# Gate products in pages of 512 columns with four buffers, paced by half weight pages at first, and readout pages read back half a page later

## Chip, cores and metric

The kernel runs on one NeuronCore of a Trainium2 chip. The metric is the device time of one execution in microseconds; 2185.92 is the median of three runs before the change. An execution is also profiled, and all rows below come from that one profiled execution. Engines are named as the profile names them: PE (TensorE), PEld (its weight loads), DVE (VectorE), ACT (ScalarE), POOL (GpSimd), SP (SyncE, which here only issues DMAs).

## The reference, cut to what matters

One layer of a hybrid block over 512 latent tokens (and 256 context tokens), D = 2048, DFF = 5632:

```
s_c = silu(c);  mx = split(s_c @ w_ada + b_ada, 6)          # six gate / shift / scale vectors of 2048
h   = modulate(rms_norm(x), mx[0], mx[1]);  u = h @ w_in    # also for the context, SSM columns only
pool groups: windowed means of u[:1536] - u, then @ w_pool
SSM groups:  B_bar u, bidirectional scan (context gives the start state), readout with C
mix = concat(pool, gelu(ssm) * sigmoid(gelu(ssm) @ w_glu)) @ w_out
x   = x + mx[2] * rms_norm(mix)
f   = conv_glu_ffn(modulate(rms_norm(x), mx[3], mx[4])) ;  x = x + mx[5] * rms_norm(f)
```

All large products are made in float32 precision from pairs of fp32r values (a high part and a remainder), three matmuls for one.

## The kernel before, in words

**Weight pages.** Every weight matrix is streamed in pages of 128x1024 floats (512 KB) in one fixed list. `Stream.get` hands out page i. Ahead of that, it makes page i+1 (an ACT copy to `whi` at L77, and a DVE subtraction to `wlo` at L78) and issues the load of page i+2 on SP (L60). The ring holds two raw pages, two `whi` and two `wlo`; so the load of page i+2 waits until `wlo` of page i is made, and `wlo` of page i+1 until PE is through with page i-1. Pages are counted here from 0 in the order of the list: 8 to 31 are w_in for the pool channels (`ub`), 40 to 65 are w_out and w_glu (`wo`, `glu`), 66 to 73 the last quarter of w_out (`wo2`, made into `wbh` and `wbl` up to three pages ahead), then w_up and w_down. A `wo` page is 24 matmuls of 128x512.

**Background threads.** Everything else is written as Python generators that `Threads.tick` steps between the matmuls of a page, twice or more a page, until a budget of microseconds (the first number that a generator yields) is used up. The second number is a lag: the thread isn't stepped again before so many pages have passed. A low priority number goes first. The steps only fix the order of instructions on each engine's queue; each engine then works its queue strictly in order, and SP does so too.

**Gate products.** Gates mx[2], mx[3], mx[4] (c = 0, 1, 2) are made as dot products on DVE: `gemv` (L963), thread of lowest priority, loads rows of w_ada as pages `gv` of 128x1024 (512 KB, SP, L172, two buffers) and multiplies each with `srow` in one SCALAR_TENSOR_TENSOR that sums into `gacc` (L972). The load of page x+1 stands just ahead of dot x, and must wait until dot x-1 has freed its buffer. The first 7 rows of c = 0 come another way (`gpair_dot`, L607); `gemv` makes 82 dots. Gate mx[5] is made likewise in the FFN stage (`gemv5`, 32 dots, L1253), one page apart and not loaded ahead.

**Readout of the SSM.** `front` (thread of priority 0) runs the SSM. Its last part is a loop over u (L845, eight groups), one half of an iteration for each half weight page:

```
        for u in range(11):
            if u < 8:
                eb_mm(u)
            if 1 <= u <= 8:
                mi_load(u - 1)
            if 2 <= u <= 9:
                y_mm(u - 2)
```

After a yield of half a page the second half follows: `window(u+1)` (ACT, from POOL's `cl`, feeds `eb_mm(u+1)`), `e_out(u)`, `y_act`, `cl_build(u+2)` (SP loads `cu` and `du`, DVE and POOL products). `e_out(u)` copies the bank to `E` (ACT), adds `du` on DVE (L828) and writes `E` to DRAM (`e_scratch`, ACT's queue); `mi_load(u)` (L832) reads it back in another layout on SP as `Mi`, and so waits on SP until the write has landed; `y_mm(u)` on PE uses `Mi`.

**Stages.** 0 to 172 us: statistics, modulation, SSM input products. 172 to 372: w_in pages with pooling, scan on DVE. 372 to 595: w_out pages, with readout (435 to 531) and gate products. 595 to 720: `wo2`, first norm, start of w_up. From 720: FFN, 1463 us.

Of the kernel before, what the change touches and what calls it, by code (L numbers as in the profile page):

```python
# [21 lines left out]
F32 = mybir.dt.float32  # L22
# [4 lines left out]
OP = mybir.AluOpType  # L27
# [102 lines left out]
def emit(tc, A, out, xs_dram, dbg=None):  # L130
    nc = tc.nc
    V, S, PO, PE = nc.vector, nc.scalar, nc.gpsimd, nc.tensor
# [4 lines left out]
    ring = es.enter_context(tc.tile_pool(name="ring", bufs=1))  # L137
# [22 lines left out]
    def pg(name, shape=(1024,), dt=F32, parts=128):  # L160
        return shaped(sb.tile([128, 1024], dt, name=name, tag="pg", bufs=NPG), shape, slice(0, parts))

    def bank(name, cols=512, parts=128):
        t = ps.tile([128, 512], F32, name=name, tag="bank")
        return t[:parts, :cols]

    def cst(name, shape, dt=F32):
        return sb.tile(shape, dt, name=name, tag=name)

    def gvload(ap, q=None):  # L170
        r = ring.tile([128, 1024], F32, name="gv", tag="gv", bufs=2)
        nc.sync.dma_start(r[:], ap)  # L172
        return r

# [42 lines left out]
    pa = phA.enter_context(tc.tile_pool(name="pa", bufs=1))  # L217
# [8 lines left out]
    srow = pa.tile([128, 2048], F32, name="srow")  # L226
    ident = cst("ident", [128, 128])
    nc.scalar.dma_start(ident[:], A["ident"])
    pscol = cst("pscol", [128, 12])
    rcnt = cst("rcnt", [128, 4, 16])  # L230
    hmask = cst("hmask", [128, 16])
    sbr = pg("sbr", (2, 32, 16))
    BBt = pa.tile([128, 1040], F32, name="bb")
# [10 lines left out]
    scr = cst("scr", [128, 1024], BF)  # L244
# [188 lines left out]
        early.setdefault(r, []).append(f)  # L433

    ada = {}
    gacc = cst("gacc", [128, 2, 4, 16])

    def ada_round(R):

# [127 lines left out]
    def mi_build(k, t, tmp):  # L567
        g0 = 4 * k
        m = t.rearrange("p (r g i h) -> p r g i h", r=2, g=4, i=8)
        for _ in cmul_build(m[:, 0], m[:, 1], BB[:, 0, g0:g0 + 4, :], BB[:, 1, g0:g0 + 4, :], PIN, g0, 4, PO, tmp):  # L570
            pass
        return m
# [31 lines left out]
    def gpair_dot(nt):  # L604
        g = gpair.pop(nt)
        for hf in range(2):
            V.scalar_tensor_tensor(scr[:], g[:, hf], 1.0, srow[:, hf * 1024:(hf + 1) * 1024], op0=OP.mult,  # L607
                                   op1=OP.mult, accum_out=gacc[:, hf, 0, nt:nt + 1])

    NGP = 7  # L610
    at(31, cond_rows)
# [68 lines left out]
    def front():  # L680
        def mi_next(k):
            if k < 8:
                cm = pb.tile([128, 512], F32, name="cm", tag="cm", bufs=1)
                mis[k] = mi_build(k, pb.tile([128, 1024], F32, name="mi", tag="mi", bufs=1)[:], cm[:])

        for gb in range(4):
# [5 lines left out]
                                        ap=[[768, 8], [6144, 16], [1, 768]]), uc.rearrange("p i c -> p (i c)"))  # L692
        mi_next(NMT)
        yield 0.0, 1.0
        for gb in range(4):
            u = pg(f"UT{gb}", (8, NCH))
            UT[gb] = u
            nc.sync.dma_start(u, bass.AP(tensor=u_dram.tensor, offset=gb * 128 * 768,
                                         ap=[[96, 8], [6144, 16], [768, 8], [1, 96]]))
            yield 0.0, 0.5 if gb < 3 else 0.75  # L700
        for gb in range(4):
            for kk in range(2):
                k = 2 * gb + kk
                g0 = 4 * k
                if k >= NMT:
                    for r in range(2):
                        mt_half(k, r)
                    mi_next(k + 1)
                    yield 0.0, 0.4
                mt = mts.pop(k)  # L710
                for r in range(2):
                    bp = bank("bp", 4 * NCH)
                    for g in range(4):
                        PE.matmul(bp[:, g * NCH:(g + 1) * NCH], mt[:, r, g, :], UT[gb][:, (g0 + g) % 8, :],
                                  start=True, stop=True)
# [116 lines left out]
        def mi_load(u):  # L832
            Mis[u] = mi = pc.tile([128, 4, 8, 16], F32, name="Mi", tag="Mi", bufs=2)
            nc.sync.dma_start(mi[:].rearrange("p g j h -> p g (j h)"),
                              bass.AP(tensor=e_dram.tensor, offset=u * 32 * 960,
                                      ap=[[16, 8], [960, 16], [240, 4], [1, 128]]))
# [8 lines left out]
        for u in range(11):  # L845
            if u < 8:
                eb_mm(u)
            if 1 <= u <= 8:
                mi_load(u - 1)
            if 2 <= u <= 9:  # L850
                y_mm(u - 2)
            if u >= 4 and u % 2 == 0:
                yt_mm(u // 2 - 2)
            yield 0.0, 0.5
            if u < 7:
                window(u + 1)
# [103 lines left out]

    gv_state = [0]

    def gemv():  # L963
        todo = [(c, n, hf) for c in range(3) for n in range(16) for hf in range(2)][2 * NGP:]
        tiles = []
        for x in range(len(todo)):

            while len(tiles) < min(x + 2, len(todo)):
                c, nt, hf = todo[len(tiles)]
                tiles.append(gvload(A["ada_n"][c, nt, hf]))  # L970
            c, nt, hf = todo[x]
            V.scalar_tensor_tensor(scr[:], tiles[x][:], 1.0, srow[:, hf * 1024:(hf + 1) * 1024], op0=OP.mult,  # L972
                                   op1=OP.mult, accum_out=gacc[:, hf, c, nt:nt + 1])
            tiles[x] = None
            gv_state[0] = 2 * NGP + x + 1
            if nt == 15 and hf == 1:
                gfin(c)
            yield 1.4, 0

    def gfin(c):  # L980
        a = acol[:, c, :]
        V.tensor_tensor(a, gacc[:, 0, c, :], gacc[:, 1, c, :], op=OP.add)
        V.tensor_tensor(a, a, bcol[:, 2 + c, :], op=OP.add)
        if c in (0, 3):
            V.tensor_tensor(a, a, gcol[:, 1 if c == 0 else 3, :], op=OP.mult)
# [68 lines left out]
    def second_half():  # L1054

        bg.finish(phs["scan"], fr_t)
        pcx["es"].close()
        P3["es"] = ExitStack()
        P3["p"] = p3 = P3["es"].enter_context(tc.tile_pool(name="p3", bufs=1))
        P3["arow"] = [t.rearrange("p (a b) -> p a b", a=2) for t in (BBt[:, :1024], PIOt[:])]  # L1060
        while gv_state[0] < 32:
            bg._step(gv_t)
        glu()
        P3["ar_t"] = bg.add(rows_of(0, P3["arow"], p3, "dg", 1), 0)

# [179 lines left out]
    def gemv5():  # L1245
        for hf in range(2):
            sr = p2.tile([128, 1024], F32, name="srow2", tag="srow2", bufs=1)
            nc.sync.dma_start(sr[:], A["c_row"][:, hf * 1024:(hf + 1) * 1024])
            S.activation(sr[:], sr[:], AF.Silu)
            for nt in range(16):  # L1250
                r = gvload(A["ada_n"][3, nt, hf])
                yield 0.0, 1
                V.scalar_tensor_tensor(scr[:], r[:], 1.0, sr[:], op0=OP.mult, op1=OP.mult,  # L1253
                                       accum_out=gacc[:, hf, 3, nt:nt + 1])
                yield 1.2, 0
        gfin(3)
        yield from rows_of(3, frow, p2, "srow2", 1)

# [133 lines left out]
    r = None  # L1392
    for t in range(4):
# [25 lines left out]
        r = rows_rstd(st8[:, t:t + 1, :], 0, 4)[0]  # L1419
# [88 lines left out]
```

## Time and profile before

| | before |
|---|---|
| median of 3 runs (lowest, highest) | 2185.92 us (2182.75, 2189.2) |
| the profiled execution's own time | 2184.42 us |
| its span, first to last instruction | 2182.6 us |
| PE busy | 2073.6 us (95%) |
| DVE busy | 1545.1 us (71%) |
| ACT / POOL busy | 690.7 / 261.7 us |
| mean granted PE clock | 0.978 |
| bytes read from HBM | 302.46 MB |

Busy is the time in which an engine had an instruction under way. The granted clock is the share of full speed (2.4 GHz) that PE got; in a stretch between 0.5 and 1 it is a mean over 1.2 and 2.4 GHz.

### The profile page before, as it was taken

How to read it: one execution, taken by the hardware profiler on the slowest of the kernel's cores; microseconds unless marked ns; L12 is line 12 of the kernel's file. 1: busy time of each engine (PE TensorE's matmuls, PEld its weight loads, DVE VectorE, ACT ScalarE, POOL GpSimd, SP SyncE). 2: the span in 40 equal slices, each digit the busy share in tenths (PEclk: the TensorE clock that was granted, in tenths of full speed). 3: DMA queues.
4: the chain of work that ended last, by engine and by line, in shares of the span. 5: the costliest groups of instructions: out<-in, count | busy, mean ns of one | idle time of the engine just before them, and what ended most of it. 6: DMA issues, size and time to landing. Idle time of an engine off the chain costs nothing.

```text
span 2182.6 us, 24482 instructions
## 1 busy us (share of the span) xinstructions
PE 2073.6 (95%) x9468; PEld 1639.6 (75%) x9468; DVE 1545.1 (71%) x2135; ACT 690.7 (32%) x969; POOL 261.7 (12%) x318
## 2 busy tenths in 40 slices
PE   7997999788798999999999999999999999999996
PEld 3576877566587888888888888888888888888885
DVE  1576899655667688767777777777766767767676
ACT  4343325433256323322222222222222222222224
POOL 5951100262016000000000000000000000000004
PEclk8899999899998999999999999999999999999998
DMA  9877423666656233333333433333322322333225
GB/s 380 302 285 258 167 85 121 211 186 193 211 205 229 68 97 116 118 123 116 123 110 116 135 116 117 125 114 114 102 90 93 97 95 90 96 96 97 90 95 192
DMA packets 94292, 315.00 MB, mean 144 GB/s; under 512 B 16992, under 2 KB 22880, under 8 KB 89952
## 3 DMA queue, kind: packets, MB, share of 16 engines
q1 hardware_dynamic: 90848, 306.07, 42.3%
q10 hardware_dynamic: 3328, 7.37, 0.9%
q8 instruction: 74, 1.21, 0.2%
q14 instruction: 42, 0.34, 0.0%
HBM read 302.46 MB, written 10.94 MB: 144 GB/s over the span
## 4 chain that ended last, share of the span: by engine, by line
PE 74%; DMA 10%; DVE 10%; issue 3%; ACT 3%; POOL 1%; SPq 0%; ACTq 0%; DVEq 0%; POOLq 0%
PE up L176 14%; PE up L178 14%; PE up L177 14%; PE dn L178 7%; PE dn L177 7%; PE dn L176 7%; DMA gv<-in_ada_n 5%; DVE wlo L78 2%; DVE scr L972 2%; DVE sct L664 1%; PE ada L446 1%; DVE B L665 1%; DMA e_scratch<-E 1%; ACT scr L1086 1%; DMA raw<-in_w_up 1%
## 5 line engine op out<-in xcount | busy, mean ns | idle before, releaser
L78 DVE TENSOR_TENSOR wlo<-raw,whi 128x1024 fp32r<-128x1024 f32 (+1 forms) x326 | 407.3, 1250 | 362.8 <-ACT whi L77 359.8
L77 ACT ACTIVATE whi<-raw 128x1024 fp32r<-128x1024 f32 (+1 forms) x326 | 341.4, 1048 | 795.0 <-PE dn L178 313.2
L1274 DVE SCALAR_TENSOR_TENSOR cv<-zp,wconv,cv 128x512 f32<-128x512 f32 x704 | 528.1, 750 | 18.8
L176 PE MATMUL up<-h,whi 128*128 128x512 f32 x1344 | 531.4, 395 | 0.0
L177 PE MATMUL up<-h,whi 128*128 128x512 f32 x1344 | 530.8, 395 | 0.0
L178 PE MATMUL up<-h,wlo 128*128 128x512 f32 x1344 | 530.8, 395 | 0.0
L178 PEld LDWEIGHTS up<-h,wlo 128*128 128x128 f32 x1344 | 251.9, 187 | 61.8
L177 PEld LDWEIGHTS up<-h,whi 128*128 128x128 f32 x1344 | 251.9, 187 | 61.5
L176 PEld LDWEIGHTS up<-h,whi 128*128 128x128 f32 x1344 | 251.9, 187 | 61.4
L178 PE MATMUL dn<-whi,g 128*128 128x512 f32 x672 | 265.5, 395 | 0.0
L176 PE MATMUL dn<-whi,g 128*128 128x512 f32 x672 | 265.5, 395 | 0.0
L177 PE MATMUL dn<-wlo,g 128*128 128x512 f32 x672 | 265.5, 395 | 0.0
L1088 POOL TENSOR_TENSOR facc<-facc,frow 128x512 f32<-128x512 f32 x11 | 15.4, 1423 | 1434.9 <-ACT scr L1086 1434.9
L972 DVE SCALAR_TENSOR_TENSOR scr<-gv,srow 128x1024 bf16<-128x1024 f32 x82 | 114.1, 1392 | 86.6 <-DMA gv<-in_ada_n 86.3
L1308 ACT ACTIVATE zp<-up 128x512 f32<-128x512 f32 x84 | 50.5, 601 | 378.6 <-PE up L178 378.6
L177 PEld LDWEIGHTS dn<-wlo,g 128*128 128x128 f32 x672 | 126.0, 187 | 30.8
L178 PEld LDWEIGHTS dn<-whi,g 128*128 128x128 f32 x672 | 126.0, 187 | 30.8
L176 PEld LDWEIGHTS dn<-whi,g 128*128 128x128 f32 x672 | 126.0, 187 | 30.8
L177 PE MATMUL wo<-wlo,mx 128*128 128x512 f32 x192 | 81.3, 424 | 32.1 <-DVE wlo L78 32.1
L1322 DVE TENSOR_TENSOR facc<-facc,dn 128x512 f32<-128x512 f32 x144 | 92.1, 680 | 0.7 <-PE dn L178 0.7
L178 PE MATMUL ub<-hT,wlo 128*128 128x512 f32 x192 | 77.2, 402 | 11.9 <-DVE wlo L78 11.9
L176 PE MATMUL wo<-whi,mx 128*128 128x512 f32 x192 | 80.5, 419 | 0.0
(276 smaller groups left out, 2441.9 us busy)
## 6 DMA issues: line engine op xcount, KB each, us to landing
raw<-in_w_up SPq DMA_DIRECT2D x176, 512.0 KB, 3.6
gv<-in_ada_n SPq DMA_DIRECT2D x114, 512.0 KB, 4.5
raw<-in_w_down SPq DMA_DIRECT2D x88, 512.0 KB, 3.6
adak<-in_ada_k SPq DMA_DIRECT2D x32, 1024.0 KB, 8.6
raw<-in_w_out SPq DMA_DIRECT2D x32, 512.0 KB, 5.0
raw<-in_w_inp SPq DMA_DIRECT2D x24, 512.0 KB, 4.9
adag<-in_ada_n SPq DMA_DIRECT2D x7, 1024.0 KB, 8.7
xl<-in_xT SPq DMA_DIRECT2D x8, 512.0 KB
```

Of the source, the lines that this page charges most:

```text
L77: nc.scalar.activation(hi[:, :n], raw[:, :n], AF.Copy)
L78: nc.vector.tensor_tensor(lo[:, :n], raw[:, :n], hi[:, :n].bitcast(F32), op=OP.subtract)
L176: PE.matmul(o, ahi, bhi, start=start, stop=False)
L177: PE.matmul(o, ahi, blo, start=False, stop=False)
L178: PE.matmul(o, alo, bhi, start=False, stop=stop)
L446: PE.matmul(ada[q, w][32 * g:32 * g + 32, :], scol[:, 4 * j + g, :], t[:, g, :], start=j == 0, stop=j == 3)
L664: V.tensor_tensor(tv, y[:, :, r], p[:, sl].unsqueeze(1).to_broadcast([128, n, 2, 32]), op=OP.mult)
L665: V.tensor_tensor(x, x, tv, op=OP.add)
L972: V.scalar_tensor_tensor(scr[:], tiles[x][:], 1.0, srow[:, hf * 1024:(hf + 1) * 1024], op0=OP.mult, op1=OP.mult, accum_out=gacc[:, hf, c, ...
L1274: V.scalar_tensor_tensor(a[:], zz, wcol, a[:], op0=OP.mult, op1=OP.add)
L1308: S.activation(zp[j][i % 2][:, 1:9, 1:65], o.rearrange("p (r c) -> p r c", r=8), AF.Copy)
L1322: V.tensor_tensor(f, f, os[t], op=OP.add)
```

## The change

`gv` pages have 512 columns (256 KB), four buffers, and are loaded three pages ahead of their dot. `gacc` has four columns of partial sums for each output instead of two; it is cleared at the start, and `gfin` has one more addition. A step of `gemv` is a half-size dot with a cost of 0.68; until the front thread has made its last `mi` page (k == 7) it also has a lag of half a weight page, afterwards none. `gemv5` uses the same generator, half a page apart. `mi_load(u - 1)` moves from the first half of iteration u to the head of its second half. `rcnt` moves to the pool that is closed ahead of the FFN.

```
-    def gvload(ap, q=None):
-        r = ring.tile([128, 1024], F32, name="gv", tag="gv", bufs=2)
+    gv_lag = [0.5]
+
+    def gvload(ap):
+        r = ring.tile([128, 512], F32, name="gv", tag="gv", bufs=4)
         nc.sync.dma_start(r[:], ap)
...
-    gacc = cst("gacc", [128, 2, 4, 16])
+    gacc = cst("gacc", [128, 4, 4, 16])
+    V.memset(gacc[:], 0.0)
...
                     mi_next(k + 1)
+                    if k == 7:
+                        gv_lag[0] = 0
                     yield 0.0, 0.4
...
             if u < 8:
                 eb_mm(u)
-            if 1 <= u <= 8:
-                mi_load(u - 1)
             if 2 <= u <= 9:
                 y_mm(u - 2)
...
             yield 0.0, 0.5
+            if 1 <= u <= 8:
+                mi_load(u - 1)
...
+    def gv_dots(todo, row):
+
         tiles = []
         for x in range(len(todo)):
...
+            while len(tiles) < min(x + 4, len(todo)):
+                c, nt, qf = todo[len(tiles)]
+                tiles.append(gvload(A["ada_n"][c, nt, qf // 2][:, qf % 2 * 512:qf % 2 * 512 + 512]))
+            c, nt, qf = todo[x]
+            V.scalar_tensor_tensor(scr[:, :512], tiles[x][:], 1.0, row(qf), op0=OP.mult,
+                                   op1=OP.mult, accum_out=gacc[:, qf, c, nt:nt + 1])
             tiles[x] = None
+            yield x
+
+    def gemv():
+        todo = [(c, n, qf) for c in range(3) for n in range(16) for qf in range(4)][4 * NGP:]
+        for x in gv_dots(todo, lambda qf: srow[:, qf * 512:(qf + 1) * 512]):
...
-            yield 1.4, 0
+            yield 0.68, gv_lag[0]
...
+        V.tensor_tensor(gacc[:, 0:2, c, :], gacc[:, 0:2, c, :], gacc[:, 2:4, c, :], op=OP.add)
```

The order of instructions on each engine shows what the steps make of it. On SP, in the readout, two rounds of the loop stand in the queue before as follows (`raw` a weight page, `Mi` the read-back, `gv` gate pages, `cu` and `du` the operands of `cl_build`):

```order
L60 DMA raw<-in_w_out 128x1024
L834 DMA Mi<-e_scratch 128x4x128
L172 DMA gv<-in_ada_n 128x1024 x2
L790 DMA cu<-in_ssm_c 128x2x64
L792 DMA du<-in_ssm_d 128x16
L60 DMA raw<-in_w_out 128x1024
L834 DMA Mi<-e_scratch 128x4x128
```

and in the changed kernel:

```order
L174 DMA gv<-in_ada_n 128x512 x4
L60 DMA raw<-in_w_out 128x1024
L839 DMA Mi<-e_scratch 128x4x128
L795 DMA cu<-in_ssm_c 128x2x64
L797 DMA du<-in_ssm_d 128x16
L174 DMA gv<-in_ada_n 128x512 x5
L60 DMA raw<-in_w_out 128x1024
L839 DMA Mi<-e_scratch 128x4x128
```

Gate pages still stand behind `Mi`, but each is loaded three dots ahead. On DVE, the same rounds before:

```order
L78 TENSOR_TENSOR wlo<-raw,whi 128x1024
L972 SCALAR_TENSOR_TENSOR scr,gacc<-gv,srow 128x1024 x2
L828 TENSOR_TENSOR E<-E,du 128x16
L800 TENSOR_TENSOR cm<-cu,pio 128x512
L802 TENSOR_TENSOR cm<-cu,pio 128x512
L78 TENSOR_TENSOR wlo<-raw,whi 128x1024
```

and in the changed kernel:

```order
L78 TENSOR_TENSOR wlo<-raw,whi 128x1024
L833 TENSOR_TENSOR E<-E,du 128x16
L805 TENSOR_TENSOR cm<-cu,pio 128x512
L807 TENSOR_TENSOR cm<-cu,pio 128x512
L976 SCALAR_TENSOR_TENSOR scr,gacc<-gv,srow 128x512 x5
L78 TENSOR_TENSOR wlo<-raw,whi 128x1024
```

The addition into `E` now stands ahead of the round's dots, right behind `wlo`. The third place is DVE in the `wo2` stage (`macc` the running sums that take a `wq` bank); before:

```order
L78 TENSOR_TENSOR wbl<-raw,wbh 128x1024
L972 SCALAR_TENSOR_TENSOR scr,gacc<-gv,srow 128x1024
L78 TENSOR_TENSOR wbl<-raw,wbh 128x1024
L972 SCALAR_TENSOR_TENSOR scr,gacc<-gv,srow 128x1024 x2
L982 TENSOR_TENSOR acol<-gacc 128x16
...
L78 TENSOR_TENSOR wbl<-raw,wbh 128x1024
L1085 TENSOR_TENSOR macc_2862<-macc_2862,wq_4441 128x512
L1085 TENSOR_TENSOR macc_2863<-macc_2863,wq_4442 128x512
L78 TENSOR_TENSOR wbl<-raw,wbh 128x1024 x2
```

and in the changed kernel:

```order
L78 TENSOR_TENSOR wbl<-raw,wbh 128x1024
L976 SCALAR_TENSOR_TENSOR scr,gacc<-gv,srow 128x512 x3
L78 TENSOR_TENSOR wbl<-raw,wbh 128x1024
L976 SCALAR_TENSOR_TENSOR scr,gacc<-gv,srow 128x512 x4
L78 TENSOR_TENSOR wbl<-raw,wbh 128x1024
L1096 TENSOR_TENSOR macc_2870<-macc_2870,wq_4640 128x512
L1096 TENSOR_TENSOR macc_2871<-macc_2871,wq_4641 128x512
L976 SCALAR_TENSOR_TENSOR scr,gacc<-gv,srow 128x512 x2
L78 TENSOR_TENSOR wbl<-raw,wbh 128x1024
```

Gate dots now go on through the whole stage. Counted from the order in full pages of 1024 columns (two half pages are one), the gate dots lie as follows:

| weight pages made | 9 to 19 | 41 to 48 | 49 to 56 | 57 to 63 | 66 to 75 |
|---|---|---|---|---|---|
| before | 20 | 20 | 17 | 19 | 6 |
| after | 10 | 21.5 | 17.5 | 19 | 14 |

## Rows read from the trace of the kernel before

**Rows 1.** Windows by stage: length, busy PE, PEld, DVE, ACT, POOL (instructions), clock, DMA share, GB/s.
```profile
172.00:262.00 90.00, 80.25 (x410) 66.64 (x409) 64.07 (x105) 35.34 (x74) 19.45 (x12) 0.96 0.67 224
371.58:435.34 63.76, 48.72 (x199) 36.73 (x197) 38.88 (x51) 32.82 (x40) 16.04 (x14) 0.89 0.62 207
435.34:530.50 95.16, 76.36 (x467) 56.40 (x467) 52.94 (x69) 35.73 (x66) 46.00 (x30) 0.95 0.63 180
530.50:594.95 64.45, 55.13 (x251) 43.62 (x250) 37.70 (x57) 19.19 (x26) 0.00 (x0) 0.94 0.66 223
594.95:636.70 41.75, 38.21 (x177) 31.54 (x176) 28.72 (x50) 18.39 (x28) 5.09 (x4) 0.96 0.68 231
720.00:2182.60 1462.60, 1444.28 (x6242) 1162.50 (x6240) 1073.74 (x1416) 393.49 (x498) 24.44 (x15) 1.00 0.34 110
```

**Rows 2.** Waits of PE, 172 to 600 us: total us, times, longest us.
```profile
PE wo L177 <- DVE wlo L78: 32.1, 12, 7.8
PE ub L178 <- DVE wlo L78: 11.9, 5, 7.6
PE eb L822 <- ACT R L814: 4.6, 5, 1.5
```

**Rows 3.** Timeline of DVE, gate dots of page 43: start, duration; in brackets the wait.
```profile
380.16 1.23 DVE L972 SCALAR_TENSOR_TENSOR scr<-gv,srow 128x1024 bf16<-128x1024 f32 x1
...
385.81 1.23 DVE L972 SCALAR_TENSOR_TENSOR scr<-gv,srow 128x1024 bf16<-128x1024 f32 x1 [1.31 <-DMA gv<-in_ada_n]
```

**Rows 4.** DMA issues, 372 to 600 us: count, KB each, us to landing.
```profile
gv<-in_ada_n SPq DMA_DIRECT2D x56, 512.0 KB, 4.4
```

**Rows 5.** DMA issues of the page's part 6, whole execution.
```profile
raw<-in_w_up SPq DMA_DIRECT2D x176, 512.0 KB, 3.6
...
raw<-in_w_pool SPq DMA_DIRECT2D x4, 192.0 KB, 2.3
```

**Rows 6.** Groups of DVE, 172 to 262 us: busy us, mean ns, idle before.
```profile
L913 DVE SCALAR_TENSOR_TENSOR p<-ps,up 128x512 f32<-128x512 f32 x5 | 3.5, 691 | 0.1
...
L972 DVE DVE_READ_ACCUMULATOR scr<-gv,srow 128x1 f32 x20 | 1.6, 80 | 0.0
```

**Rows 7.** Windows of pages 42 to 45, 46, 47 and 48, 60 to 63; columns as rows 1.
```profile
371.58:403.83 32.25, 26.27 (x111) 20.24 (x109) 19.26 (x30) 23.93 (x24) 1.82 (x4) 1.00 0.67 225
403.83:418.05 14.22, 7.32 (x24) 5.53 (x24) 7.28 (x12) 4.36 (x8) 6.71 (x8) 0.78 0.61 203
418.05:435.34 17.29, 15.12 (x64) 10.96 (x64) 12.34 (x14) 4.52 (x10) 7.52 (x4) 0.79 0.54 177
551.83:587.50 35.67, 27.63 (x117) 21.31 (x115) 20.51 (x31) 6.12 (x6) 0.00 (x0) 0.98 0.75 250
```

**Rows 8.** Chain that ended last, readout, 450 to 520 us: start, us, what.
```profile
451.14 6.37 DMA e_scratch<-E
...
477.01 3.80 DMA e_scratch<-E
...
481.62 5.93 DMA gv<-in_ada_n
...
487.63 1.24 DVE scr L972 x2
...
514.10 6.66 DMA e_scratch<-E
```

**Rows 9.** Timelines of SP, DVE and ACT, 180 to 191 us.
```profile
180.47 1.32 SPq L60 DMA_DIRECT2D raw<-in_w_inp  x1
...
186.95 1.23 DVE L972 SCALAR_TENSOR_TENSOR scr<-gv,srow 128x1024 bf16<-128x1024 f32 x1 [6.94 <-DMA gv<-in_ada_n]
...
190.27 1.06 ACT L77 ACTIVATE whi<-raw 128x1024 fp32r<-128x1024 f32 x1 [8.28 <-DMA raw<-in_w_inp]
```

**Rows 10.** Chain that ended last, 505 to 535 us.
```profile
520.82 7.38 DMA Mi<-e_scratch
```

**Rows 11.** Chain that ended last, `wo2` stage.
```profile
622.77 0.73 ACT scr L1086 x2
```

More of the change, by code (lines that the diff above doesn't have):

```diff
@@ L229, in emit @@
     pscol = cst("pscol", [128, 12])
-    rcnt = cst("rcnt", [128, 4, 16])
+    rcnt = pa.tile([128, 4, 16], F32, name="rcnt")
     hmask = cst("hmask", [128, 16])
@@ L607, in gpair_dot @@
             V.scalar_tensor_tensor(scr[:], g[:, hf], 1.0, srow[:, hf * 1024:(hf + 1) * 1024], op0=OP.mult,
-                                   op1=OP.mult, accum_out=gacc[:, hf, 0, nt:nt + 1])
+                                   op1=OP.mult, accum_out=gacc[:, 2 * hf, 0, nt:nt + 1])
     NGP = 7
@@ L961, in emit @@
     gv_state = [0]
-    def gemv():
-        todo = [(c, n, hf) for c in range(3) for n in range(16) for hf in range(2)][2 * NGP:]
+    def gv_dots(todo, row):
         tiles = []
         for x in range(len(todo)):
[L968 to L973, printed above, removed]
-            tiles[x] = None
-            gv_state[0] = 2 * NGP + x + 1
-            if nt == 15 and hf == 1:
+            while len(tiles) < min(x + 4, len(todo)):
[4 more added lines that the diff above has]
+                                   op1=OP.mult, accum_out=gacc[:, qf, c, nt:nt + 1])
+            tiles[x] = None
+            yield x
+    def gemv():
+        todo = [(c, n, qf) for c in range(3) for n in range(16) for qf in range(4)][4 * NGP:]
+        for x in gv_dots(todo, lambda qf: srow[:, qf * 512:(qf + 1) * 512]):
+            c, nt, qf = todo[x]
+            gv_state[0] = 4 * NGP + x + 1
+            if nt == 15 and qf == 3:
                 gfin(c)
-            yield 1.4, 0
+            yield 0.68, gv_lag[0]
     def gfin(c):
         a = acol[:, c, :]
+        V.tensor_tensor(gacc[:, 0:2, c, :], gacc[:, 0:2, c, :], gacc[:, 2:4, c, :], op=OP.add)
         V.tensor_tensor(a, gacc[:, 0, c, :], gacc[:, 1, c, :], op=OP.add)
@@ L1060, in second_half @@
         P3["arow"] = [t.rearrange("p (a b) -> p a b", a=2) for t in (BBt[:, :1024], PIOt[:])]
-        while gv_state[0] < 32:
+        while gv_state[0] < 64:
             bg._step(gv_t)
@@ L1249, in gemv5 @@
             S.activation(sr[:], sr[:], AF.Silu)
[L1250 to L1255, printed above, removed]
+            todo = [(3, nt, 2 * hf + q) for nt in range(16) for q in range(2)]
+            for x in gv_dots(todo, lambda qf: sr[:, qf % 2 * 512:qf % 2 * 512 + 512]):
+                yield 0.8, 0.5
         gfin(3)
```

## Prediction

> **What bounds the kernel now.** I read the windows by stage first, then PE's waits, then DVE's and SP's timelines where PE waits, and last the chain that ended last. From 720 us on PE is busy 1444 of 1463 us at full clock [rows 1]: nothing that leaves PE's work alone can gain there, and 389 us of DVE's time are free. Between 172 and 595 us it is otherwise. In the four stages from 172 us and from 372 to 595 us PE stands idle 9.8, 15.0, 18.8 and 9.3 us, and its clock is 0.96, 0.89, 0.95 and 0.94 [rows 1]. Nearly all of it is a wait for a weight page's `wlo` on DVE [rows 2], and DVE is late for three different reasons.
>
> First, the gate ring. In pages 42 to 45, DVE is busy only 19.3 of 32.3 us [rows 7], since each dot waits for its page: 5.65 us for two dots [rows 3], which is a landing of 4.4 us [rows 4] and a dot of 1.23, with the load issued only when the dot before has freed a buffer. Three dots a page make 8.1 us of a weight page whose matmuls take PE 26.3 / 4 = 6.6 us at most [rows 7]. Pages 60 to 63 are the same.
>
> Second, the readout is a closed ring. `e_scratch` is written, SP waits for it at `Mi`, the gate page stands behind `Mi` on SP, the dot behind the gate page, the addition into `E` behind the dot, and then `e_scratch` is written again: in one round 3.8 us, 5.9 us and 1.2 us, and the short steps between. From 451.14 to 514.10 us that is five rounds of 12.6 us [rows 8], while PE has 76.4 us of work for the eight pages of the stage [rows 1], 9.5 us each.
>
> Third, at 180 us DVE waits 6.9 us for a gate page, and PE then 7.6 us [rows 2, 9].
>
> **The change part by part.** *Price of a half dot.* A STT of 128x512 takes 0.69 us and the accumulator's read 0.08 [rows 6], so about 0.75 us start to start (below: half of 1.27, above: 0.83). Two cost 1.50 instead of 1.27 us.
>
> *Landing of a half page.* 512 KB land in 3.6 us, 192 KB in 2.3 us [rows 5], so 256 KB in 2.6 us by a straight line. Gate pages of 512 KB in the crowded stretch need 0.8 us more [rows 4, 5]; with as many bytes under way as before I take 2.6 + 0.8 = 3.4 us. Bounds: 2.6, and 4.4 if halving wins nothing. Four buffers then give four dots in 3.4 + 0.75 + 0.1 = 4.25 us, 1.06 us a half dot, where a full dot takes 2.8 us now.
>
> *First pages (172 to 262 us).* Half as many dots, with four half pages loaded ahead; the dots of pages 9 and 10 find theirs landed, so the wait of 6.9 us on DVE and with it the 7.6 us on PE go [rows 2, 9]. Of the clock's loss behind the stall (0.04 of 90 us, 3.6 us [rows 1]) I take 1.4: **-9 us**. Late next is the weight page behind: its load was issued at 180.47 us, held up by gate loads, and its `whi` began at 190.27 after a wait of 8.3 [rows 9], with more dots and their waits ahead of its `wlo`. The load now waits for the first dot only, some 3 us less, and its `wlo` has one pair of landed dots ahead; so this page comes earlier by about as much as PE does. Bounds: -5 (two thirds of the stall) and -11.
>
> *Pages 42 to 48.* Pages 42 to 45 hold 6, 7, 6 and 7 half dots: 26 x 1.06 = 27.6 instead of 32.25 us [rows 7], just above PE's 26.3: -4.7. Page 46 holds two half dots ahead of its `wlo` instead of two full ones with their waits: -2.3 of 14.2; its wait for `cu` and POOL stays. Pages 47 and 48: 13 x 1.06 and 1.5 as an allowance for DVE's longer times beside POOL, 15.3 of 17.3: -2. Sum **-9 us**; bounds 0 (landing 4.4) and -15 (all of PE's idle time).
>
> *Readout (435 to 531 us).* Gate pages are now loaded three dots ahead of use, and `E` stands ahead of the dots, so `Mi` has the write of a whole page earlier to wait for and the ring is cut. What is left is PE's 76.4 us [rows 1] and waits that are not of the ring, such as those for `R` of 4.6 us [rows 2]: 81.5 of 95.2 us, **-13.5 us**. DVE has 52.9 us busy there, and 35 half dots for 17 full ones add 35 x 0.75 - 17 x 1.27 = 4.7 us: not the bound. Bounds: -5 and -18.8.
>
> *Pages 57 to 64.* Pages 60 to 63 hold 25 half dots, 26.5 us; PE has 27.6 of the 35.7 us [rows 7]: -8. With the idle time there the lowered clock of the stage, 0.94 [rows 1], recovers a little, 1 us: **-9 us**; bounds -3 and -11.
>
> *The `wo2` stage (595 to 637 us).* What was not done early comes late: 28 half dots for 6 full ones, 28 x 0.75 - 6 x 1.27 = +13.4 us on DVE. Three times a dot stands behind two squares on ACT, since both write `scr`: 3 x 2 x 0.73 [rows 11] = +4.4. DVE is idle 13.0 of 41.8 us here [rows 1], but in pieces, waiting for weight pages that SP now issues behind gate loads. Behind DVE wait `wbl`, and the norm that PE has to wait for. I take **+6 us**; bounds 0 (PE is up to three pages behind `wbl`) and +18 (none of the idle time is of use).
>
> *At no cost.* The FFN's 32 dots become 64, +7.4 us on DVE, beside 389 us of its idle time [rows 1]; uncovered they would cost those 7.4. The 114 more issues on SP stand among waits that SP has anyway, for buffers and for `e_scratch`; where one is in the way it is in the 0.1 us that I added to the landing above. The clearing of `gacc`, four additions of 32 columns and `rcnt`'s place: nothing.
>
> Sum: -9 - 9 - 13.5 - 9 + 6 = -34.5 us; against the profiled execution's own time of 2184.4 (its span is 1.8 less, and the median of the runs 1.5 more) **2150 us**. All terms moved a third of the way to their bounds give 2143 to 2163.
>
> **The rivals.** *Halving wins no landing time (2167).* If 256 KB land in 4.4 us, a half dot takes 1.31 us: pages 42 to 48 gain about 0 (34.1 for 32.25, less page 46), pages 60 to 63 gain 3 (32.8 for 35.7), the late stage costs 8; -9 + 0 - 13.5 - 3 + 8 = -17.5, 2167. For it speaks that the DMA share is 0.75 in pages 60 to 63 [rows 7]; against it that 192 KB land in 2.3 us. The Trainium skill, "DMA: Bandwidth & Descriptors", § Rules for kernel authors, speaks against the change in this sense: it asks for at least 1 MiB in a DMA for full bandwidth. By that rule this rival would be the case; the rows on landing agree that a smaller page lands at fewer bytes a microsecond, but not that it lands as late.
>
> *All of PE's idle time closes (2129).* -9 - 15 - 18.8 - 9.3, and 0.21 of 17.3 us of clock in pages 47 and 48 [rows 7], 3.6; nothing lost late: -55.7. For it speaks that DVE has the time; against it the waits for POOL, `cu` and `R`, which the change leaves.
>
> *Halving wins little and the late stage jams (2177).* The first rival with the late stage at +18: -7.5 us, at the edge of no change.
>
> *Slower: `Mi` comes too late for PE (2203).* `Mi` is issued half a page later, and has landed up to 7.4 us after its issue [rows 10]. If SP reaches it only when PE is at the same place, each of eight rounds shows these 7.4 us on top of PE's 9.5: 16.9 us instead of 95.2 / 8 = 11.9, so +40, and the readout's gain is gone: -9 - 9 - 9 + 6 + 40 = +19. It decides from 5 us shown a round. Against it: DVE and SP run about a page ahead of PE, and half a page of matmuls and `eb` lie between; for it: SP stands behind four gate loads, each released by a dot.
>
> **How the numbers follow.** Forecast 0.54; no landing time won 0.17; all closes 0.15; jam 0.05; `Mi` late 0.09. The likeliest is 2150. A range from 2124 to 2171 leaves out the last two and some of the second's spread, about 0.2 in all. About 0.3% (6.5 us) is what a measurement of this kernel can tell from no change: 2179 to 2192 is the same. Faster 0.87 (the first three and a little of the jam), same 0.04, slower 0.09.
>
> **What the profile after would show.** Right: dots of 0.69 us, gate landings near 3.4 us; no wait for `gv` at 180 us; weight pages 42 to 45 about 6.9 us apart; in the readout SP hardly waiting for `e_scratch`, pages about 10 us apart; more DVE work and less idle time from 595 to 637 us, PE reaching the FFN some 35 us earlier, and a FFN of the same length. What would make it wrong: landings near 4.4 us; PE waiting for `Mi` at `yb`; a gap on PE ahead of the first `uh` that grew by more than 10 us.

## The result: slower, and the profile after

The changed kernel takes 2204.47 us (median of 4 runs, 2203.9 to 2210.56) against 2184.35 us for the kernel before (median of 4 runs): a ratio of 1.0095, 95% interval 1.0070 to 1.0119. The forecast was 2150 us, range 2124 to 2171.

| | after |
|---|---|
| the profiled execution's own time | 2204.39 us |
| its span | 2202.6 us |
| PE busy | 2083.7 us (95%) |
| DVE busy | 1578.5 us (72%) |
| ACT / POOL busy | 690.6 / 255.8 us |
| mean granted PE clock | 0.973 |

Windows of the changed kernel follow, columns as in [rows 1]. The stretches are the same weight pages as there: the bounds were moved with the `wlo` of the weight page that stands at them, and PE can be further behind it in one kernel than in the other.

```profile
172.00:253.50 81.50, 80.58 (x417) 66.98 (x416) 61.10 (x108) 35.47 (x74) 18.82 (x12) 1.00 0.57 188
364.63:430.75 66.12, 50.56 (x220) 37.64 (x218) 44.14 (x100) 32.50 (x40) 14.83 (x14) 0.90 0.68 218
430.75:535.20 104.45, 80.11 (x449) 62.18 (x449) 65.16 (x103) 36.07 (x66) 40.55 (x30) 0.84 0.56 162
535.20:600.53 65.33, 58.05 (x256) 44.90 (x256) 42.26 (x100) 20.07 (x28) 0.00 (x0) 0.97 0.74 234
600.53:652.24 51.71, 44.71 (x192) 35.79 (x193) 37.98 (x82) 17.26 (x26) 5.98 (x4) 0.93 0.77 251
739.80:2202.60 1462.80, 1444.39 (x6242) 1162.65 (x6240) 1077.70 (x1481) 393.52 (x498) 24.45 (x15) 0.99 0.34 110
```

The first stretch ends at 253.5 where before it ended at 262: that gain came. The pages from 42 to 48 are 2.4 us longer than before (63.76), the readout 9.3 longer (95.16), pages 57 to 64 are 0.9 longer (64.45), and the `wo2` stage is 10 longer (41.75). Between these stretches, pages 20 to 41 are 1.5 us longer, and the way from the end of the `wo2` stage to the FFN is 4.3 longer. The FFN is as long as before.

The waits of the changed kernel between 430.75 and 535.20 us (total us, times, longest) show what the readout waits for now; of each engine's rows those that matter:

```profile
SPq L174 <- DVE scr L976: 65.7, 25, 9.1
...
SPq L839 <- DMA e_scratch<-E: 0.7, 1, 0.7
...
PE yb L765 <- DMA Mi<-e_scratch: 19.3, 7, 7.6
...
DVE cm L805 <- DMA cu<-in_ssm_c: 27.1, 6, 7.7
```

The same rows of the kernel before, 435.34 to 530.50 us:

```profile
SPq L834 <- DMA e_scratch<-E: 47.2, 8, 7.8
SPq L172 <- DVE scr L972: 11.3, 6, 4.1
...
PE wo L177 <- DVE wlo L78: 8.7, 6, 2.3
PE yb L760 <- DMA Mi<-e_scratch: 5.4, 1, 5.4
...
DVE cm L800 <- DMA cu<-in_ssm_c: 7.9, 5, 2.4
```

SP hardly waits for `e_scratch` any more: the old ring is cut. But SP now waits 65.7 us for dots to free a gate buffer, DVE 27.1 us for `cu`, and PE 19.3 us for `Mi`. That is a ring again. One round of it is seen in the timelines of the changed kernel (start, duration; the wait in brackets), first DVE's:

```profile
477.97 0.69 DVE L805 TENSOR_TENSOR cm<-cu,pio 128x512 f32<-128x512 f32 x1 [5.51 <-DMA cu<-in_ssm_c]
...
479.21 1.58 DVE L976 SCALAR_TENSOR_TENSOR scr<-gv,srow 128x512 bf16<-128x512 f32 x1
...
480.84 1.46 DVE L976 SCALAR_TENSOR_TENSOR scr<-gv,srow 128x512 bf16<-128x512 f32 x1
...
482.34 1.64 DVE L976 SCALAR_TENSOR_TENSOR scr<-gv,srow 128x512 bf16<-128x512 f32 x1
...
484.02 1.65 DVE L976 SCALAR_TENSOR_TENSOR scr<-gv,srow 128x512 bf16<-128x512 f32 x1
...
491.62 1.64 DVE L805 TENSOR_TENSOR cm<-cu,pio 128x512 f32<-128x512 f32 x1 [1.36 <-DMA cu<-in_ssm_c]
```

and SP's queue in the same round:

```profile
484.01 0.33 SPq L174 DMA_DIRECT2D gv<-in_ada_n  x1
484.43 0.38 SPq L60 DMA_DIRECT2D raw<-in_w_out  x1
484.91 0.63 SPq L839 DMA_DIRECT2D Mi<-e_scratch  x1
485.64 0.56 SPq L795 DMA_DIRECT2D cu<-in_ssm_c  x1
...
486.95 13.05 SPq L174 DMA_DIRECT2D gv<-in_ada_n  x5
```

The products `cm` start when `cu` has landed (477.97); four dots stand behind them; the gate load at 484.01 waits for the third of these dots; `Mi` and the next `cu` stand behind that load on SP (484.91, 485.64); that `cu` lets `cm` start at 491.62. The round takes 13.65 us, 7.67 from `cm` to the issue of `cu` and 5.98 from there to the next `cm`. PE's work for a page took 9.5 us in the kernel before. In this round, which begins behind a wait of 3.8 us for `Mi`, PE is busy 13.25 us at a granted clock of 0.80, a mean over 1.2 and 2.4 GHz:

```profile
477.97:491.62 13.65, 13.25 (x77) 10.66 (x77) 9.62 (x14) 5.85 (x11) 6.96 (x7) 0.80 0.52 152
```

Over the whole readout the clock is 0.84 (0.95 before). PE's own work takes 80.1 us there instead of 76.4, and its waits make 24.3 us instead of 18.6.

### The profile page after: what moved, and what is told of

Read it like the earlier page. It is cut to its first block, busy times and chain, and to the rows that moved or that the text cites. A ratio compares the mean times of both kernels' runs of the same rounds, so it can differ in the third digit from the quotient of the medians.

```text
span 2202.6 us, 25052 instructions
## 1 busy us (share of the span) xinstructions
PE 2083.7 (95%) x9468; PEld 1646.6 (75%) x9468; DVE 1578.5 (72%) x2368; ACT 690.6 (31%) x969; POOL 255.8 (12%) x318
## 4 chain that ended last, share of the span: by engine, by line
PE 74%; DMA 9%; DVE 8%; issue 4%; ACT 3%; POOL 1%; SPq 1%; DVEq 0%; ACTq 0%; POOLq 0%
PE up L178 14%; PE up L180 14%; PE up L179 14%; PE dn L179 7%; PE dn L180 7%; PE dn L178 7%; DMA gv<-in_ada_n 3%; DVE wlo L78 1%; DVE scr L976 1%; PE ada L449 1%; DMA Mi<-e_scratch 1%; PE ub L180 1%; PE ub L178 1%; PE ub L179 1%; ACT scr L1097 1%
## 5 line engine op out<-in xcount | busy, mean ns | idle before, releaser
L78 DVE TENSOR_TENSOR wlo<-raw,whi 128x1024 fp32r<-128x1024 f32 (+1 forms) x326 | 401.6, 1232 | 364.3 <-ACT whi L77 361.3
L1282 DVE SCALAR_TENSOR_TENSOR cv<-zp,wconv,cv 128x512 f32<-128x512 f32 x704 | 528.1, 750 | 18.8
L976 DVE SCALAR_TENSOR_TENSOR scr<-gv,srow 128x512 bf16<-128x512 f32 x228 | 187.5, 822 | 50.4 <-DMA gv<-in_ada_n 40.2
L178 PE MATMUL wo<-whi,mx 128*128 128x512 f32 x192 | 80.1, 417 | 0.1
```

Of the source, the lines that this page charges most:

```text
L78: nc.vector.tensor_tensor(lo[:, :n], raw[:, :n], hi[:, :n].bitcast(F32), op=OP.subtract)
L178: PE.matmul(o, ahi, bhi, start=start, stop=False)
L976: V.scalar_tensor_tensor(scr[:, :512], tiles[x][:], 1.0, row(qf), op0=OP.mult, op1=OP.mult, accum_out=gacc[:, qf, c, nt:nt + 1])
L1282: V.scalar_tensor_tensor(a[:], zz, wcol, a[:], op0=OP.mult, op1=OP.add)
```

## Experiments

The start of `wlo` in DVE's timeline, page by page, tells where each run gained or lost. The table holds the change of the time between two such starts against the kernel before, in us, for one profiled execution each; the last column runs to page 76, the first behind `wo2` whose `wlo` waits for the norm.

| run | to page 20 | 20-42 | 42-49 | 49-57 | 57-64 | 64-76 | median us | ratio to before (95%) |
|---|---|---|---|---|---|---|---|---|
| after | -8.5 | +1.5 | +2.4 | +9.3 | -1.1 | +16.2 | 2204.5 | 1.0095 (1.0070, 1.0119) |
| a_mi_first | -9.3 | 0.0 | +2.9 | 0.0 | -8.3 | +16.1 | 2190.7 | 1.0036 (1.0022, 1.0049) |
| a_lag0 | +4.7 | +0.4 | +4.1 | +9.9 | +2.8 | +0.3 | 2206.6 | 1.0102 (1.0087, 1.0118) |
| a_mi_lag0 | +2.6 | +0.2 | +0.6 | -1.7 | +0.3 | +0.8 | 2189.1 | 1.0026 (1.0016, 1.0036) |
| b_mi_later | -2.0 | +1.6 | +1.8 | -2.2 | +6.2 | -1.6 | 2186.7 | 1.0011 (1.0001, 1.0021) |
| a_cu_early | -7.8 | +1.6 | +3.9 | -17.0 | -0.8 | +15.6 | 2178.7 | 0.9978 (0.9969, 0.9988) |
| a_cu_mi | -6.9 | +1.4 | +5.9 | -12.7 | -7.8 | +18.0 | 2180.4 | 0.9981 (0.9970, 0.9992) |
| a_cl_dve | -7.6 | +1.6 | -0.4 | +12.9 | +1.2 | +13.9 | 2204.4 | 1.0092 (1.0076, 1.0107) |
| a_2x512 | +1.5 | +1.5 | +24.9 | +17.1 | +18.3 | +28.2 | 2276.7 (one run) | |
| a_cu_nolate | -9.2 | +1.5 | +4.2 | -17.0 | +0.7 | -5.5 | 2161.1 | 0.9896 (0.9882, 0.9909) |
| b_cu_early | +0.2 | 0.0 | +0.7 | -4.3 | +1.6 | -1.2 | 2182.6 | 0.9996 (0.9987, 1.0005) |
| b_cu_mi_later | -0.1 | +1.4 | +1.3 | -18.8 | +2.9 | -0.3 | 2172.3 | 0.9948 (0.9935, 0.9962) |
| b_best_6 | +1.4 | +2.3 | +0.9 | -20.3 | -0.7 | +3.5 | 2170.6 | 0.9941 (0.9927, 0.9954) |

**Undoing the parts: a_mi_first, a_lag0, a_mi_lag0, b_mi_later.** The first three undo the move of `mi_load` (first diff), the lag (second diff), or both, in the changed kernel; the fourth makes the move of `mi_load` alone in the kernel before.

```
                 eb_mm(u)
+            if 1 <= u <= 8:
+                mi_load(u - 1)
             if 2 <= u <= 9:
...
             yield 0.0, 0.5
-            if 1 <= u <= 8:
-                mi_load(u - 1)
```

```
-    gv_lag = [0.5]
+    gv_lag = [0]
```

> The changed kernel with the read-back of Mi put back into the first half of an iteration; all else as changed (2204 us). Theory 1, the read-back comes too late for PE: the 19.3 us that PE waits for Mi at yb between 435 and 535 us go and most of them are won, 2204 - 15 = about 2189. Theory 2, the rounds are held by cu, whose load stands on SP behind gate loads that wait for dots that stand on DVE behind the products of cu: PE's wait only changes its name, SP waits for e_scratch again, and the readout stays at 100 us or more, 2198 to 2208.

> The changed kernel without the pacing by half a weight page (the lag is 0 from the start), so about 17 half dots of every 10 weight pages are done early again and the last gate dot stands at weight page 69 instead of 75. Theory 3, the dots that were not done early are what the wo2 stage pays for: from page 64 to the first uh the changed kernel lost 16 us to before, of which some 12 come back, while the first pages lose up to 7 of the 8 us won there: 2204 - 12 + 7 = 2199 or less. If the pacing is worth its price: 2204 or more, with the wo2 stage as long as before.

> Both of these undone: only the page of 512 columns, four buffers and the loads three dots ahead are left of the change. If the two act apart, the two gains add: theories 1 and 3 together give 2204 - 15 - 5 = about 2184, theories 2 and 3 give about 2199. If small pages with four buffers are worth by themselves what I forecast for the gate ring, this is the fastest of the four, under 2180.

> The kernel before (2184 us) with the read-back of Mi alone moved to the second half of an iteration. Theory 1: PE waits for Mi in each round, 2184 + 10 to 19 = 2194 to 2203. Theory 2: the move by itself does no harm, since the long way of SP to cu comes from the gate loads; it cuts the wait of 47.2 us for e_scratch and gives 2178 to 2188.

With `Mi` first again 14 us come back, the time that the first theory gave; but SP waits for `e_scratch` again, as the second theory gave. And the same move alone in the kernel before costs 0.1%, where that theory asked for 10 to 19 us. So the later read-back is not harmful by itself; it is so together with the half gate pages. The readout waits of a_mi_first (428.98 to 524.18 us, PE and SP) and of b_mi_later (436.73 to 529.66) show what takes its place:

```profile
PE eb L827 <- ACT R L819: 15.1, 10, 5.1
...
SPq L839 <- DMA e_scratch<-E: 35.5, 7, 6.8
```

```profile
PE yb L760 <- DMA Mi<-e_scratch: 10.1, 5, 4.4
...
SPq L172 <- DVE scr L972: 57.2, 11, 11.8
```

In the first, SP waits for `e_scratch` and PE for `R`, which comes from `cu`: the readout is as long as before (0.0). In the second, the new ring stands in the kernel before too, and is about as long as the old one. Here is its round, on DVE of b_mi_later, 12.28 us with two full dots:

```profile
469.61 0.69 DVE L800 TENSOR_TENSOR cm<-cu,pio 128x512 f32<-128x512 f32 x1 [5.31 <-DMA cu<-in_ssm_c]
...
472.89 2.13 DVE L972 SCALAR_TENSOR_TENSOR scr<-gv,srow 128x1024 bf16<-128x1024 f32 x1
...
481.89 0.69 DVE L800 TENSOR_TENSOR cm<-cu,pio 128x512 f32<-128x512 f32 x1 [1.55 <-DMA cu<-in_ssm_c]
```

The lag was expected to cost 12 us late and to win up to 7 early. Taking it away returned 15.9 us late (+0.3 for +16.2), but lost 13.2 us early (+4.7 for -8.5): the time is the same. What the pacing wins at first is paid back in the `wo2` stage. With both undone, the half pages with four buffers are left, and they cost 0.26%. Its 2189.1 us lie between the two sums of theories (2184 and 2199), and the forecast of under 2180 in case small pages pay by themselves did not come true.

**Cutting the new ring: a_cu_early, a_cu_mi.** The loads of `cu` and `du` become a function of their own, called one iteration ahead; a_cu_mi has `Mi` first as well.

```
+        def cu_load(u):
...
+            cds[u] = (cu, du)
         def cl_build(u):
+            cu, du = cds.pop(u)
...
             if u + 2 < 8:
                 cl_build(u + 2)
+            if u + 3 < 8:
+                cu_load(u + 3)
```

> The changed kernel (2204 us) with the loads of cu and du issued one iteration earlier, behind the products of the iteration ahead of theirs; Mi stays where the change put it. Theory 2 (a new ring: cu's load stands on SP behind gate loads that each wait for a dot, and the dots stand on DVE behind the products that wait for cu): DVE's wait for cu, 27.1 us between 435 and 535, falls under 8, a round falls from 13.5 us to 10 to 11, PE's wait for Mi of 19.3 us falls under 6, and 12 to 16 us are won: about 2190. Theory 1 (half a page later is simply too late for Mi): DVE's wait goes, but PE's wait for Mi stays at 12 us or more: 2198 to 2206.

> The same early loads of cu and du, and Mi read back in the first half of an iteration, as before the change. If the ring through cu is all, PE's wait for R of 15.1 us in the run with Mi first goes as well, and 6 to 9 us are won on that run: 2182 to 2185. If SP's wait for e_scratch (35.5 us in that run) is the next ring, nothing is won on it: 2188 to 2192.

The changed kernel gains 26 us by this alone, where I had expected 12 to 16, and is then 0.22% faster than the kernel before. The readout of a_cu_early, the same work as the third window above, and its largest waits on PE and SP:

```profile
432.99:511.14 78.15, 70.36 (x443) 54.56 (x436) 60.43 (x103) 35.47 (x66) 36.23 (x27) 0.93 0.75 216
```

```profile
PE yb L765 <- DMA Mi<-e_scratch: 7.4, 2, 5.8
...
SPq L174 <- DVE scr L985: 35.2, 27, 5.2
```

The readout falls from 104.45 to 78.15 us, 3 less than I had forecast for the change, with `Mi` where the change put it. DVE has no wait for `cu` left among its rows, and PE's wait for `Mi` falls from 19.3 to 7.4 us (I expected under 6). This is the test that separates the theories: the lateness of `Mi` came from the ring through `cu`. With `Mi` first (a_cu_mi) the readout loses 4 us of the 17, and pages 57 to 64 give 7 back; the time is the same within the intervals, a little better than either expectation. SP still waits 37.0 us for `e_scratch` there, and the whole is no slower for it, so that wait alone was no measure of a loss.

**The dots beside POOL: a_cl_dve.**

```
-            PO.tensor_tensor(cl[0], xr, pr, op=OP.mult)
+            V.tensor_tensor(cl[0], xr, pr, op=OP.mult)
...
-            PO.tensor_tensor(cl[0], cl[0], ts[0], op=OP.subtract)
+            V.tensor_tensor(cl[0], cl[0], ts[0], op=OP.subtract)
```

(and the same for `cl[1]`).

> The changed kernel with POOL's four products and sums of cl_build made on DVE, so that POOL works on du alone in the readout. Theory 4, a dot beside POOL is held for the length of a POOL instruction, whatever its own size: half dots of the readout, median 1.58 us in the changed kernel, fall to 0.69, and DVE's busy time there stays about the same (28 more instructions of 0.69 against 33 dots that are 0.6 shorter). The time moves little, since DVE's way from cu to the last dot only shortens from 7.9 to 7.2 us a round: 2196 to 2206. If something else slows the dots (a crowded SBUF, DMA writes), they stay at 1.3 us on the mean, and the time rises by 8 x 2.8 us on DVE: 2215 or more.

The dots of the readout by form: before (435.34 to 530.50 us), after (430.75 to 535.20) and in a_cl_dve (430 to 535); count | busy us, mean ns | idle before:

```profile
L972 DVE SCALAR_TENSOR_TENSOR scr<-gv,srow 128x1024 bf16<-128x1024 f32 x18 | 30.0, 1666 | 26.8 <-DMA gv<-in_ada_n 26.8
```

```profile
L976 DVE SCALAR_TENSOR_TENSOR scr<-gv,srow 128x512 bf16<-128x512 f32 x36 | 44.8, 1245 | 7.0 <-DMA gv<-in_ada_n 6.0
```

```profile
L976 DVE SCALAR_TENSOR_TENSOR scr<-gv,srow 128x512 bf16<-128x512 f32 x34 | 23.4, 689 | 7.6 <-DMA gv<-in_ada_n 6.8
```

With POOL's products out of the readout a half dot takes 0.69 us there as everywhere: POOL was what slowed it. The time is unchanged, as expected. I put that down to the products, which stand on DVE now, ahead of the dots and in the same ring (DVE's wait for `cu` is 36.8 us here); this was not tested apart. So this run shows the cause of the longer dots, not what they are worth in the end.

**Bytes under way: a_2x512.** Two buffers and one load ahead, in place of four and three.

```
-        r = ring.tile([128, 512], F32, name="gv", tag="gv", bufs=4)
+        r = ring.tile([128, 512], F32, name="gv", tag="gv", bufs=2)
...
-            while len(tiles) < min(x + 4, len(todo)):
+            while len(tiles) < min(x + 2, len(todo)):
```

> The changed kernel with two gate buffers of 512 columns, loaded one dot ahead, so half as many bytes under way. If a page of 256 KB lands in 4.3 us whatever is under way with it, two dots take 4.3 + 0.75 + 0.1 us and weight pages 42 to 45 with their 26 half dots 67 us. If the landing follows the bytes under way, it falls to 2.6 to 3.0 us and the four pages take 45 to 50 us. Both are far over the 32 us of the kernel before and of the changed one, and the time is 2300 us or more.

Pages 42 to 45 of this run, and the waits of its dots in them:

```profile
374.65:424.48 49.83, 34.51 (x116) 26.19 (x114) 23.40 (x63) 23.94 (x24) 1.86 (x4) 0.83 0.57 180
```

```profile
DVE scr L976 <- DMA gv<-in_ada_n: 26.3, 25, 1.8
```

49.83 us is what the second expectation gave; the whole, 2276.7 us, stayed under the 2300 that I had expected. From the issue on SP to the start of the dot, for the 13 dots between 364 and 402 us that waited over 0.15 us, the median is 3.0 us (2.5 to 4.1). More buffers, the other direction, were not tried.

**The late dots: a_cu_nolate.** a_cu_early without the 28 half dots behind weight page 65, so that parts of the gate mx[4] are not computed.

```
+        todo = todo[:-29] + todo[-1:]
```

> The run with cu and du loaded early (2178.7 us), with the 28 half dots left out that stand behind weight page 65 (parts of the gate mx[4] are not computed; all else as it was). Theory 3, these late dots on DVE and their loads on SP are what the wo2 stage and the first norm lose against before: from page 64 to the first uh 15.6 us come back, 2163 to 2166. If the stage is longer for another reason (the order of other work, the shared scr, weight loads that come late anyway): less than 6 us, 2173 or more.

The `wo2` stage of this run, and PE's wait for the norm in it:

```profile
577.26:611.40 34.14, 31.71 (x155) 26.57 (x155) 20.24 (x31) 17.34 (x26) 5.10 (x4) 1.00 0.60 196
```

```profile
PE h2p L1168 <- DVE macc L1106: 0.7, 1, 0.7
```

In the changed kernel, and in the kernel before, that wait was

```profile
PE h2p L1158 <- DVE macc L1096: 10.7, 2, 8.6
...
PE h2p L1147 <- DVE macc L1085: 3.2, 2, 2.8
```

17.6 us come off, 2 more than the 15.6 expected: the late dots hold up `wbl` and the last sums into `macc`, and so the norm for which PE waits. The run takes away the dots on DVE and their loads on SP together; which of the two does the harm was not separated.

**The same edits with full pages: b_cu_early, b_cu_mi_later, b_best_6.** The kernel before with `cu_load` as above, then with `mi_load` in the second half too, then also with a lag behind the first six dots:

```
-            yield 1.4, 0
+            yield 1.4, 0.5 if x < 6 else 0
```

> The kernel before (2184 us; full pages of 1024 columns, Mi in the first half of an iteration) with the loads of cu and du issued one iteration earlier, nothing else. There DVE waits only 7.9 us for cu, and SP's ring goes through e_scratch (47.2 us): by theory 2 little is won, 2179 to 2185. If early loads of cu are worth as much without the change (26 us in the changed kernel): 2160 to 2170.

> The kernel before with both: cu and du loaded early, and Mi read back in the second half of an iteration; gate pages stay at 1024 columns with two buffers. By theory 2 both rings of the readout are cut, and the readout wins 12 to 17 us as in the changed kernel with early cu, without the late dots: 2167 to 2173. If three half pages loaded ahead are needed for it, SP stands at the gate loads as in the run with Mi alone moved (58.5 us there) and 2179 to 2186 is left.

> The kernel before with early cu and du and the later read-back of Mi (2172.3 us), and in addition a lag of half a weight page behind each of the first six full gate dots, which puts two dots instead of three behind the wlo of page 9 and 9 instead of 6 dots into the wo2 stage. If the stall at 180 us comes from the third dot, whose page is loaded only when the first dot has freed a buffer, DVE's wait of 6.3 us there goes and some 6 us are won up to page 20, of which 3 to 4 us are lost to the late dots: 2168 to 2171. If the late dots cost as much each as the half dots of the changed kernel did per 256 KB (0.6 us), nearly all is kept less 3.6 us: the same number; if the stage has no room at all: 2173 or more.

`cu` early alone does nothing (0.9996), `Mi` later alone nothing (1.0011), both together 0.52%: each leaves one of the two rings closed. The readout of b_cu_mi_later, with PE at full clock:

```profile
438.10:514.47 76.37, 70.05 (x457) 53.17 (x456) 53.47 (x68) 38.16 (x72) 42.95 (x27) 1.00 0.68 209
```

It is as short as with half pages (78.15), and with only the 6 late dots of before the whole is 6 us faster than a_cu_early. The lag in b_best_6 took the stall at 180 us away (page 10 starts 7.3 us earlier than before), but by page 20 all of it is lost again, and the time is that of b_cu_mi_later within the intervals. It lies in the expected 2168 to 2171, but by luck: nothing of the gain up to page 20 was kept. These two are the fastest complete versions.

## Why the prediction was wrong

The forecast took 34.5 us off; the span grew by 20.0. Three steps failed: that cutting the ring through `e_scratch` leaves no ring in the readout, that a half page lands in 3.4 us, and that a half dot costs 0.75 us also beside POOL. The late dots had the right mechanism and too small a price. Where a term below has its own stretch, the bounds are those of the windows above.

**First pages, -9: measured -8.5.** The size was right. The reason was right only in part: b_best_6 removed the stall and kept nothing of it at page 20, with 18 full dots in these pages for before's 20; a_lag0, with 38 half dots, lost 4.7. The changed kernel has 20 half dots there, and by these runs it is that smaller number, more than the end of the stall, that gains.

**Pages 42 to 48, -9: measured +2.4.** Two steps failed. One is the landing of 3.4 us for 256 KB, in pages 42 to 45. I had put these pages at 4.7 us less; they took 32.03 us for 32.25, with 26 half dots, 1.23 us each where I had 1.06. Their window, and that of pages 60 to 63:

```profile
364.63:396.66 32.03, 29.00 (x116) 22.40 (x114) 23.02 (x61) 23.87 (x24) 1.87 (x4) 0.95 0.83 270
558.45:591.09 32.64, 28.11 (x117) 21.30 (x115) 21.70 (x55) 5.83 (x6) 0.00 (x0) 1.00 0.80 263
```

DVE waited in pages 42 to 45 as follows (total us, times, longest):

```profile
DVE scr L976 <- DMA gv<-in_ada_n: 8.3, 7, 2.8
```

Two of these dots, and the issues of their pages on SP four dots earlier:

```profile
369.15 0.69 DVE L976 SCALAR_TENSOR_TENSOR scr<-gv,srow 128x512 bf16<-128x512 f32 x1 [1.22 <-DMA gv<-in_ada_n]
...
377.67 0.69 DVE L976 SCALAR_TENSOR_TENSOR scr<-gv,srow 128x512 bf16<-128x512 f32 x1 [2.78 <-DMA gv<-in_ada_n]
```

```profile
364.85 0.43 SPq L174 DMA_DIRECT2D gv<-in_ada_n  x1
...
371.51 0.37 SPq L174 DMA_DIRECT2D gv<-in_ada_n  x1
```

These dots could start 4.3 and 6.2 us after the issue; over the seven that waited the median is 4.3 (3.1 to 6.2). Nine dots of the full pages before, taken in the same way, give 4.3 too. The seven of 26 are the late ones, though. Landings themselves, which the profiles hold only in part, have medians of 3.9 us (a_mi_lag0, 33 of them between 365 and 610 us) and 4.7 (a_cu_mi, 17) in two other runs with four half pages; the 4.4 of [rows 4] is the median of six. With two buffers it was 3.0. So the landing goes with the bytes under way, and four half pages land about as late as two full ones: for the landing, the first rival, which I gave 0.17, was near the case. Its 32.8 us for pages 60 to 63 stand against 32.64 measured; its 34.1 for pages 42 to 45 are 2 too long. The rule of the Trainium skill, "DMA: Bandwidth & Descriptors", § Rules for kernel authors, that asks for large DMAs, pointed the right way; but these runs do not show the small page to be the cause, since with fewer under way the same 256 KB land in 3.0 us.

The other step is in pages 46 to 48: forecast 4.3 us shorter, they were 2.6 longer (34.09 for 31.51). In page 46, DVE waits for `cu`, with no dots left to do beside the wait:

```profile
DVE cm L805 <- DMA cu<-in_ssm_c: 4.8, 1, 4.8
```

The kernel before, with two full dots there, waited 1.9 us. I had let this wait stay as it was. Three half dots beside POOL took 1.5 to 1.8 us each as well, as below.

**Readout, -13.5: measured +9.3.** "The ring is cut" was the step that failed. It is true of `e_scratch` (SP's wait 47.2 to 0.7 us), but I did not follow SP's queue on to what stands behind the gate loads. A load three dots ahead still waits for a dot, and the dots moved behind `cm`, which waits for `cu`, which SP issues behind these loads. a_cu_early shows it: with that one link cut the readout takes 78.15 us, close to the 81.5 that I had. I had also called nearly all of PE's idle time a wait for `wlo`; of the 18.8 us in the readout it was 8.7, and 5.4 were for `Mi` already. The fourth rival put 0.09 on `Mi` coming too late for PE and gave 2203; its place was right and its price was not. PE waited 2.8 us on the mean, seven times, not 7.4 us eight times, and these waits took the place of most of those for `wlo`, so the readout grew by 9.3 us and not by 40. The rival's total agrees with the result by luck, because its terms outside the readout were 31 us too good.

The price of a half dot, 0.75 us start to start, was wrong beside POOL: 1.5 to 1.7 us in the round shown above. A full dot beside POOL had been held up by about as much in the kernel before, so each half dot pays the same hold as a full one: 36 dots took 44.8 us, where 18 had taken 30.0. Of the dots that began in the readout 8 of 17 were held before (and six `wlo`), and 22 of 35 after (and no `wlo`); DVE's time over the unhindered rose from some 13 to 20 us. I had taken the price from [rows 6], where nothing beside it held the instruction up.

**Pages 57 to 64, -9: measured +0.9** (-1.1 in the table, which ends at the start of page 64). Pages 60 to 63 gained 3.0 us, as the first rival had it. Pages 57 to 59 were 1.9 longer and page 64 was 2.0 longer. In pages 57 to 59 PE did not lack work: it was busy 22.77 of 23.25 us, with 78 `wo` matmuls where it had 66 before, work that the longer readout had left behind. In a_mi_first it had 60 there, and these pages and the next gained 8.3 us to the start of page 64.

**The `wo2` stage, +6: measured +10.0**, and +4.3 behind it, up to the FFN, where I had put nothing (the +16.2 of the table take in page 64). The mechanism was right and the size was off: with +14.2 to page 76 it came near the upper bound of 18, and without any late dots 17.6 us come back. DVE is idle 13.7 us in the stage, as I had counted on, but in waits for `wbh` (6.4), for gate pages (5.1) and for the squares (1.9), and PE's wait for the norm rose from 3.2 to 10.7 us.

**FFN, 0: measured +0.2.** Right.

What stays open: how much of the 13.65 us round is due to the longer dots alone was not separated, since taking POOL out put its products on DVE. Half pages with early `cu` and without the lag were not run, so what half pages could win beside both cut rings is not known.

## What to carry to other kernels

When a ring through a queue is cut, follow the same queue to the next link: a load "three ahead" is still released by an instruction, and everything behind it on that queue is released by it too; here neither of two edits gained anything alone, and both gained 0.5%. Halving a transfer and doubling the buffers keeps the bytes under way, and here it kept most of the landing time. Work that is paced away from a crowded stretch has to land in one with room: look for the place that it moves to before counting the gain.

## What the runs showed of the hardware

A dot on DVE that runs beside POOL's products takes about 0.9 us longer, whatever its own size. POOL's timeline in the round shown above:

```profile
478.71 1.54 POOL L806 TENSOR_TENSOR cl<-cu,pio 128x512 f32<-128x512 f32 x1
480.21 1.54 POOL L808 TENSOR_TENSOR cl<-cu,pio 128x512 f32<-128x512 f32 x1
481.71 1.71 POOL L809 TENSOR_TENSOR cl<-cl,cm 128x512 f32<-128x512 f32 x1
483.39 1.73 POOL L810 TENSOR_TENSOR cl<-cl,cm 128x512 f32<-128x512 f32 x1
```

The four dots end at 480.79, 482.30, 483.98 and 485.67 us, each 0.5 to 0.6 us behind the end of one of these four (480.25, 481.75, 483.42, 485.12): one dot for each POOL instruction. In b_mi_later a full dot beside POOL took 2.13 us instead of 1.23, 0.9 more, the same as a half dot's 1.58 instead of 0.69. POOL is held as well: with no DVE instruction beside it, such a product took 1.09 us and a sum 1.25 (changed kernel, at 404.89 and 405.95 us). The Trainium skill, "SBUF — State Buffer", § SBUF: two separate sides, says that DVE with two SBUF inputs and a GpSimd operation that reads SBUF share a port pair as an exclusive lock for a whole instruction. These rows agree that a hold comes with each instruction and not with its size; but the two times do not add up in full, since a dot and a product, 0.69 and 1.09 us alone, follow each other every 1.50 us.
